# Two decoder blocks on one core: the convolutions' first tap moves from ACT to DVE, and the small table products go six to a step

## The chip, the core and the metric

The kernel runs on one core of a Trainium2 chip. The core has a matrix engine (PE, with its weight loads listed apart as PEld), a vector engine (DVE), a scalar engine (ACT), a general engine (POOL), and SyncE (SP), which here issues the DMAs of the weights. Each engine works through its own queue of instructions in the order in which they were written; between engines, an instruction waits on semaphores. The metric is the device time of one execution in microseconds, as the median of three runs.

## The reference

Two blocks are computed one after the other on a sequence of 256 tokens of width 2048, in fp32. The first block has two layers; the change lies mostly in its feed-forward network (FFN), which each layer has, and in its first mixer.

```python
def causal_dwconv(x, w):                  # CONV_WIDTH = 3
    s = x.shape[1]
    xp = jnp.pad(x, ((0, 0), (CONV_WIDTH - 1, 0), (0, 0)))
    y = xp[:, 0:s] * w[0]
    for j in range(1, CONV_WIDTH):
        y = y + xp[:, j:j + s] * w[j]
    return y

def short_conv_mixer(x, w_in, conv_w, w_out):
    b_gate, c_gate, xv = jnp.split(x @ w_in, 3, axis=-1)
    y = b_gate * causal_dwconv(c_gate * xv, conv_w)
    return y @ w_out

def conv_ffn(x, w_up, conv_w, conv_b, w_down):     # D_FF = 5632
    h = causal_dwconv(x @ w_up, conv_w) + conv_b
    g, u = jnp.split(h, 2, axis=-1)
    return (jax.nn.silu(g) * u) @ w_down

def first_block(...):
    for layer in range(2):
        mix = short_conv_mixer(...) if layer == 0 else diff_attention(...)
        x = layer_norm(ALPHA * x + mix, ...)
        x = layer_norm(ALPHA * x + conv_ffn(x, ...), ...)
    return x
```

The second block has an attention/linear-attention layer and a layer with a state-space mixer (S5). For the latter, tables are needed that depend on parameters alone (complex powers and their products with B and C); the kernel works them out early.

## The kernel before

**Tiles.** Activations lie transposed: 128 channels on the partitions, 256 tokens along the row, 16 such tiles for the width of 2048. A weight matrix is read in tiles of 128 x 128. Each fp32 operand is split into a high and a low part, so that a product becomes `hi` x (`xhi`, `xlo`) in one matmul of 512 columns (L308) and `lo` x `xhi` in one of 256 (L302). The splitting of the weights is done on the fly, per *unit* of 8 weight tiles: SP loads `raw` (L213), ACT makes `whi` (`hi_to`, an ACT copy of 128x1024, shown under the helper's line L195), DVE makes `wlo` (`lo_to`, L238). `raw` has 3 buffers, `whi` and `wlo` have 4 each. Before the matmuls of unit c are written, `whi` of unit c+2 is; after them, `wlo` of unit c+2 is. An output tile with 16 tiles of depth takes two units; 8 pairs of matmuls each.

**Epilogues.** What happens to an output tile after its matmuls is a generator: each `yield` ends a step, and one step of each waiting generator is written after each unit (`advance`). So a `yield` between two instructions puts them a unit apart in the program. `merge` (L482 to 487) takes the 512-wide PSUM tile: ACT copies the right half into `mt`, a step later DVE adds it to the left half (L487), which frees the PSUM tile; there are three such PSUM buffers (`pmm`). In an up tile of the FFN (`epi_up`) the sum goes into `pad`, one of four padded buffers; then comes the convolution `conv3`: the first tap on ACT (`h<-pad`, with weight and bias), a step later the second and third tap on DVE (L769, L770). The tiles alternate between gate and value: of a gate tile ACT takes the SiLU (`h<-h`), of a value tile DVE multiplies with the gate's (L1069), then `glu` is split, `hi` on ACT and, a step later, `lo` on DVE (L478). In the first mixer the convolution stands in `epi_xv`.

**FFN.** Each FFN goes through its 44 pairs of up tiles in three chunks (15, 15 and 14 pairs, `FCH`), and after each chunk the chunk's part of the down product (`mm_rows`): first four output tiles at once (`mm_side`, in groups of two depth tiles), then twelve one by one. A LayerNorm (`ln.apply`) stands ahead of each FFN.

**Background.** Other generators run beside: one step of each after every unit (`run_bg`). `s5_tables` is one of them, in the list `slow`, which pauses while a LayerNorm is near (`hold`). It has eight rounds (from L967), each of: complex products `cmul` (L899) of growing size, 1, 2, 4, 8, 16 and 32 columns for each of four channels, in steps of three or two DVE instructions; two times four instructions for `bd` (L981 to L984); twelve large products of 128x512 and 128x640 one to a step; transposes and products on PE, and copies on ACT.

Of the kernel before, what the change touches and what calls it, by code (L numbers as in the profile page):

```python
# [24 lines left out]
AF = mybir.ActivationFunctionType  # L25
OP = mybir.AluOpType
AX = mybir.AxisListType

T = 256
# [114 lines left out]
def kernel(ctx: ExitStack, tc: tile.TileContext, A, out, dbg=None, upto=99):  # L144
# [52 lines left out]
    V, S, G, PE = nc.vector, Scalar(), nc.gpsimd, nc.tensor  # L197
# [55 lines left out]
    def flush():  # L253
        while pending:
            advance()
# [168 lines left out]
    def P(name, i=0, n=1):  # L424
        c, w = COL[name]
        return par[:, c + i:c + i + n]
# [55 lines left out]
    def merge(ps, dst, m=128, mul=None, fac=None):  # L482

        t = ep.tile([128, T], F32, tag="mt", name="mt")
        S.activation(t[:m], ps[:m, T:], AF.Copy)
        yield
        V.tensor_add(dst, ps[:m, :T], t[:m])  # L487
        if mul is None:
            return
        while not mul.ready:  # L490
            yield
        if fac is None:
            V.tensor_mul(dst, dst, mul.rstd[:m])
        else:
            V.scalar_tensor_tensor(dst, dst, fac, mul.rstd[:m], op0=OP.mult, op1=OP.mult)
# [268 lines left out]

    def conv3(dst, pad, w, bias=0.0):

        S.activation(dst, pad[:, 0:T], AF.Identity, scale=w[0], bias=bias)
        yield
        V.scalar_tensor_tensor(dst, pad[:, 1:T + 1], w[1], dst, op0=OP.mult, op1=OP.add)  # L769
        V.scalar_tensor_tensor(dst, pad[:, 2:T + 2], w[2], dst, op0=OP.mult, op1=OP.add)  # L770

# [12 lines left out]
    cur = {}  # L784
# [7 lines left out]
    def epi_xv(i):  # L792
        def f(ps):
            z = ep.tile([128, T], F32, tag="c1", name="c1")
            yield from merge(ps, z)
            pad = pads[i % 4]
            V.tensor_mul(pad[:, 2:], z, cur.pop(("c", i)))
            cur["y", i] = ep.tile([128, T], F32, tag="c2", name="c2")
            yield from conv3(cur["y", i], pad, [P("a_conv", j * 16 + i) for j in range(3)])
        return f  # L800

    def epi_b(i):
# [80 lines left out]
    def s5_tables():  # L883
# [7 lines left out]
        def copy(dst, src, scale=1.0):  # L891
            S.activation(dst, src, AF.Copy, scale=scale)

        def cmul(dr, di, ar, ai, br, bi, u1, u2, n=3):

            ops = ((V.tensor_mul, u1, ar, br), (V.tensor_mul, u2, ai, bi), (V.tensor_sub, dr, u1, u2),
                   (V.tensor_mul, u1, ar, bi), (V.tensor_mul, u2, ai, br), (V.tensor_add, di, u1, u2))
            for i, (f, d, x, y) in enumerate(ops):
                f(d, x, y)  # L899
                if i % n == n - 1:  # L900
                    yield 1
# [65 lines left out]
        for i in range(8):  # L967
            bc = bgp.tile([128, 4, 4, 16], F32, tag="s5bc", name="s5bc", bufs=1)
            nc.gpsimd.dma_start(bc, A["s5bc"][:, i])
            p4 = slice(4 * i, 4 * i + 4)  # L970
            copy(d0[:, :, 1:], mag4[:, p4].unsqueeze(2).to_broadcast([128, 4, 63]))
            for k in range(6):
                n = 1 << k
                fr, fi = (pq[:, r, k, p4].unsqueeze(2).to_broadcast([128, 4, n]) for r in range(2))
                v1, v2 = u1[:, :, 0, :n], u2[:, :, 0, :n]
                yield from cmul(rot[:, 0, :, n:2 * n], rot[:, 1, :, n:2 * n], rot[:, 0, :, :n], rot[:, 1, :, :n],
                                fr, fi, v1, v2, 3 if n < 16 else 2)
            cr, ci = (z[:, p4].unsqueeze(2).to_broadcast([128, 4, 16]) for z in (cor, coi))
            w1, w2 = u1[:, :, 0, :16], u2[:, :, 0, :16]
            for r in range(2):  # L980
                V.tensor_mul(w1, cr, bc[:, r])  # L981
                V.tensor_mul(w2, ci, bc[:, 1 - r])
                for ps_, cs_ in half:
                    (V.tensor_add if r else V.tensor_sub)(bd[ps_, r, :, cs_], w1[ps_], w2[ps_])  # L984
                    copy(cd[ps_, r, :, cs_], bc[ps_, 2 + r])
                yield 1
            ar, ai = (pd[:, r, p4].unsqueeze(3).to_broadcast([128, 4, 4, 32]) for r in range(2))
            br, bi = (bd[:, r].unsqueeze(2).to_broadcast([128, 4, 4, 32]) for r in range(2))
            yield from cmul(ba[:, 0], ba[:, 1], ar, ai, br, bi, u1[:, :, :4], u2[:, :, :4], 1)
            for r in range(2):  # L990
                ps = pbg.tile([128, 4, 128], F32, tag="bg", name="s5t")
                for a in range(4):
                    PE.transpose(ps[:, a, :], ba[:, r, a].rearrange("p j h -> p (j h)"), ident)
                yield 1
                S.activation(bt[:, :, r, :], ps, AF.Copy)
            nc.sync.dma_start(s5_a[i], ta)
            ar, ai = (pa[:, r, p4].unsqueeze(3).to_broadcast([128, 4, 5, 32]) for r in range(2))
            br, bi = (cd[:, r].unsqueeze(2).to_broadcast([128, 4, 5, 32]) for r in range(2))
            yield from cmul(ca[:, 0], ca[:, 1], ar, ai, br, bi, u1, u2, 1)
            copy(ca[:, 1], ca[:, 1], -1.0)  # L1000
            yield 1
            for r, u in enumerate((u1, u2)):
                copy(u[:, :, :4], bd[:, r].unsqueeze(2).to_broadcast([128, 4, 4, 32]))
                yield 1
            yield 1
            ps = pbg.tile([128, 4, 128], F32, tag="bg", name="s5k")
            for a in range(4):
                for r in range(2):
                    PE.matmul(ps[:, a, :], (u1, u2)[r][:, a, :4].rearrange("p j h -> p (j h)"),
                              ca[:, r, a, :4].rearrange("p j h -> p (j h)"), start=r == 0, stop=r == 1)  # L1010
            yield 1
            for j in range(4):
                q = slice(32 * j, 32 * j + 32)
                S.activation(km[q, :, 32 * j:], ps[q, :, :128 - 32 * j], AF.Copy)
            nc.gpsimd.dma_start(s5_b[i][:, :1024].rearrange("p (r a j h) -> p r a j h", r=2, a=4, j=4),  # L1015
                                ca[:, :, :, 1:, :])
            nc.gpsimd.dma_start(s5_b[i][:, 1024:], km.rearrange("p a c -> p (a c)"))
            yield 1
# [28 lines left out]
    def ffn(layer, which, feed, scale=None):  # L1047
        r = big_r("rf")
        ln = LayerNorm(which, r)
        hold = {}  # L1050
        for f0, nf in FCH:
            glu = big_y("glu")

            def epi_up(j, i, is_u, glu):
                def f(ps):
                    pad = pads[(2 * i + is_u) % 4]
                    yield from merge(ps, pad[:, 2:])
                    if i == 0:
                        yield
                    h = ep.tile([128, T], F32, tag=f"c{is_u}", name="h")  # L1060
                    yield from conv3(h, pad, [P("f_conv", (layer * 3 + q) * 88 + j) for q in range(3)],
                          P("f_convb", layer * 88 + j))
                    if not is_u:
                        hold[i] = h
                        yield
                        S.activation(h, h, AF.Silu)
                        return
                    yield
                    V.tensor_mul(h, h, hold.pop(i))  # L1069
                    yield  # L1070
                    yield from split_late(glu, i, h)
                return f

            epis = [epi_up(f0 + i + NFF * u, i, u, glu) for i in range(nf) for u in range(2)]
            if f0:
                for e in epis:
                    mm_tile(xs, e)
            else:
                mm_run(xs, epis, feed)
                debug(f"ln{layer}", hres)  # L1080

            def epi_dn(m, f0=f0):
                def f(ps):
                    if f0 != FCH[-1][0]:
                        residual(r, m, ps, None if f0 == 0 else r)
                        return
                    ln.take(m, ps, r)
                    if m == 8:
                        S.tables()
                    if m < 14:  # L1090
                        yield
                    yield from ln.add(m, r)
                return f

            mm_rows(glu, epi_dn, f0, nf, ln.LAST if f0 == FCH[-1][0] else KT)
        flush()
        return ln.apply(xs, scale)
# [23 lines left out]
    scale = 128.0 ** -0.5  # L1121
# [617 lines left out]
    for e, a, n in ((V, 0, 1), (G, 5, 2), (V, 1, 2), (V, 3, 2), (G, 11, 2), (V, 7, 2), (V, 9, 2), (V, 13, 2), (V, 15, 1)):  # L1739
        y = hres[:, a:a + n, :]  # L1740
# [113 lines left out]
```

## Time and profile before

| | us |
|---|---|
| median of three runs (3296.56 to 3300.56) | 3298.67 |
| profiled execution | 3297.06 |
| its span, first to last instruction | 3295.3 |
| PE busy | 3215.1 |
| DVE busy | 2369.9 |
| ACT busy | 1710.7 |
| POOL busy | 484.7 |

The busy time of an engine is the time in which it had an instruction at work. A matmul that starts on time runs beside its neighbours, so a mean duration of one is longer than its share. "Idle before, releaser" tells how long an engine stood still before an instruction and whose end released it. The granted clock of PE is given as a share of full speed. The first FFN lies between about 404 and 1130 us of the span, the second between about 1612 and 2290.

### The profile page before, as it was taken

What the parts mean: (1) busy time and instruction counts of PE and PEld (TensorE: products, weight loads), DVE (VectorE), ACT (ScalarE), POOL (GpSimd) and SP (SyncE); (2) the same over time, 40 slices, a digit from 0 to 9 for tenths busy, and PEclk for the clock granted to TensorE, in tenths of its full rate; (3) what the DMA queues carried; (4) which work ended last, traced back from release to release, by engine and by line L of the source; (5) the groups of instructions that cost most, each with busy time, mean ns of one, the idle gap of its engine ahead of it and who ended that gap; (6) DMA issues with size and microseconds to landing.
All of it is one profiled execution on the core that took longest, in us unless ns stands there. A gap on an engine that the chain in (4) does not pass through costs nothing.

```text
span 3295.3 us, 51091 instructions
## 1 busy us (share of the span) xinstructions
PE 3215.1 (98%) x18674; PEld 2829.8 (86%) x18674; DVE 2369.9 (72%) x3958; ACT 1710.7 (52%) x2624; POOL 484.7 (15%) x551
## 2 busy tenths in 40 slices
PE   9999999999999999999999999999999999999998
PEld 8888887888888888888888888888788888899887
DVE  6677877777877785766866676667876666688765
ACT  5544555455455554554555455455554565444754
POOL 4200500000000066240500000000500001121102
PEclk9999999999999999999999999999999999999999
DMA  7666556666656646545466666666454555775554
GB/s 220 196 188 208 152 178 182 201 195 189 203 186 185 195 149 191 162 151 168 146 185 189 189 189 190 189 189 188 140 173 148 160 180 184 226 254 170 150 185 149
DMA packets 245131, 599.23 MB, mean 182 GB/s; under 512 B 36592, under 2 KB 119152, under 8 KB 244880
## 3 DMA queue, kind: packets, MB, share of 16 engines
q1 hardware_dynamic: 242496, 588.37, 58.4%
q0 software_dynamic: 2208, 7.37, 0.7%
q8 instruction: 147, 2.41, 0.3%
q14 instruction: 104, 0.85, 0.1%
q10 hardware_dynamic: 176, 0.23, 0.0%
HBM read 578.04 MB, written 17.83 MB: 181 GB/s over the span
## 4 chain that ended last, share of the span: by engine, by line
PE 76%; DVE 11%; DMA 4%; ACT 4%; issue 3%; SPq 1%; POOL 0%; DVEq 0%; ACTq 0%; POOLq 0%
PE mm L308 45%; PE mm L302 24%; DVE wlo L238 6%; ACT whi L195 3%; DMA raw<-in_up_dram 2%; DMA raw<-in_cd_dram 1%; PE ml L1302 1%; DVE h L769 1%; PE mm L305 1%; PE mm L395 1%; DVE pad L487 1%; PE mm L396 1%; PE mm L394 1%; SPq L213 1%; DMA raw<-in_a_in_dram 0%
## 5 line engine op out<-in xcount | busy, mean ns | idle before, releaser
L238 DVE TENSOR_TENSOR wlo<-raw,whi 128x1024 fp32r<-128x1024 f32 (+3 forms) x1083 | 1335.1, 1234 | 693.3 <-ACT whi L195 666.6
L308 PE MATMUL mm<-xs,whi 128*128 128x512 f32 x5776 | 1415.3, 394 | 18.2 <-DVE xs L650 11.0
L195 ACT ACTIVATE whi<-raw 128x1024 fp32r<-128x1024 f32 (+3 forms) x1083 | 1120.6, 1038 | 504.3 <-PE mm L308 225.6
L308 PEld LDWEIGHTS mm<-xs,whi 128*128 128x128 f32 x5776 | 1056.1, 189 | 227.0 <-issue 14.1
L302 PEld LDWEIGHTS mm<-xs,wlo 128*128 128x128 f32 x5776 | 751.2, 191 | 58.7 <-DVE wlo L238 25.8
L302 PE MATMUL mm<-xs,wlo 128*128 128x256 f32 x5776 | 779.1, 285 | 17.1 <-DVE wlo L238 15.6
L308 PE MATMUL mm<-glu,whi 128*128 128x512 f32 x1352 | 335.0, 394 | 12.2 <-DVE pad L487 9.4
L308 PEld LDWEIGHTS mm<-glu,whi 128*128 128x128 f32 x1352 | 247.9, 190 | 59.8 <-issue 13.8
L195 ACT ACTIVATE h<-pad,par 128x256 f32<-128x256 f32 x176 | 105.6, 601 | 369.8 <-DVE pad L487 365.5
L195 ACT ACTIVATE mt<-mm 128x256 f32<-128x256 f32 x369 | 136.5, 371 | 245.8 <-PE mm L308 224.6
L302 PEld LDWEIGHTS mm<-glu,wlo 128*128 128x128 f32 x1408 | 188.2, 193 | 11.6 <-DVE wlo L238 1.3
L302 PE MATMUL mm<-glu,wlo 128*128 128x256 f32 x1408 | 192.6, 285 | 1.1 <-DVE wlo L238 1.1
L1015 POOL DMA_DIRECT2D s5b<-s5ca x8 | 7.3, 910 | 776.8 <-ACT s5ca L195 776.8
L602 POOL COPY ln_s<-rf 128x256 f32<-128x256 f32 x2 | 0.9, 434 | 715.3 <-DVE rf L578 715.3
L770 DVE SCALAR_TENSOR_TENSOR h<-pad,par,h 128x256 f32<-128x256 f32 x176 | 85.4, 485 | 6.3
L769 DVE SCALAR_TENSOR_TENSOR h<-pad,par,h 128x256 f32<-128x256 f32 x176 | 84.2, 478 | 2.3 <-ACT h L195 2.3
L487 DVE TENSOR_TENSOR pad<-mm,mt 128x256 f32<-128x256 f32 x176 | 73.4, 418 | 2.9 <-ACT mt L195 2.9
L195 ACT ACTIVATE h<-h 128x256 f32<-128x256 f32 x88 | 36.7, 417 | 45.9 <-DVE h L770 45.5
L308 PE MATMUL mm<-y_att,whi 128*128 128x512 f32 x224 | 54.6, 391 | 0.0
L308 PE MATMUL mm<-y_cd,whi 128*128 128x512 f32 x224 | 54.5, 391 | 0.0
L308 PE MATMUL mm<-y_ab,whi 128*128 128x512 f32 x224 | 54.5, 391 | 0.0
L308 PE MATMUL mm<-y_conv,whi 128*128 128x512 f32 x224 | 54.5, 391 | 0.0
(566 smaller groups left out, 3151.6 us busy)
## 6 DMA issues: line engine op xcount, KB each, us to landing
raw<-in_up_dram SPq DMA_DIRECT2D x336, 512.0 KB, 3.9
raw<-in_ab_dram SPq DMA_DIRECT2D x106, 512.0 KB, 4.0
raw<-in_a_in_dram SPq DMA_DIRECT2D x88, 512.0 KB, 4.4
raw<-in_cd_dram SPq DMA_DIRECT2D x88, 512.0 KB, 4.4
raw<-in_down_dram SPq DMA_DIRECT2D x72, 512.0 KB, 3.8
raw<-in_down_dram SPq DMA_DIRECT2D x168, 128.0 KB, 2.6
raw<-in_down_dram SPq DMA_DIRECT2D x48, 448.0 KB, 4.0
raw<-in_k_dram SPq DMA_DIRECT2D x32, 512.0 KB, 4.4
```

Source lines behind the costliest of these rows:

```text
L195: nc.scalar.activation(dst, src, func, **k)
L213: nc.sync.dma_start(r[:, c:c + nk * m], w[t, :, k0:k0 + nk, :].rearrange("p k n -> p (k n)"))
L238: V.tensor_sub(lo[:, c:c + step], r[:, c:c + step], hi[:, c:c + step].bitcast(F32))
L302: PE.matmul(ps[:m, :T], lo[:, c:c + m], x[:, kx, :T], start=False, stop=last, skip_group_check=True)
L305: PE.matmul(ps[:m, :T], hi[:, c:c + m], x[:, kx, a:a + T], start=first and a == 0, stop=last and a == T, skip_group_check=True)
L308: PE.matmul(ps[:m, :], hi[:, c:c + m], x[:, kx, :], start=first, stop=last, skip_group_check=True)
L394: PE.matmul(ps[b], xhi, whi[:, :, k, :], start=first, stop=False, skip_group_check=True)
L395: PE.matmul(ps[b], xhi, wlo[:, :, k, :], start=False, stop=False, skip_group_check=True)
L396: PE.matmul(ps[b], xlo, whi[:, :, k, :], start=False, stop=last, skip_group_check=True)
L487: V.tensor_add(dst, ps[:m, :T], t[:m])
L769: V.scalar_tensor_tensor(dst, pad[:, 1:T + 1], w[1], dst, op0=OP.mult, op1=OP.add)
L770: V.scalar_tensor_tensor(dst, pad[:, 2:T + 2], w[2], dst, op0=OP.mult, op1=OP.add)
```

## The change

The first tap of every convolution (16 in the first mixer, 88 in each of the two FFNs) is no longer an ACT instruction but a `tensor_scalar` of DVE: multiplied with the weight, the bias (or zero) added. The step boundary behind it is gone: `conv3` is a plain function, and `pad`'s sum and the three taps stand in one step, so that what follows in the generator is written one unit earlier. In `s5_tables`, the products of 1, 2 and 4 columns take one step of six instructions where they took two of three, and the two halves of `bd` stand in one step: a round has 32 steps where it had 36. The number of table instructions is the same.

```diff
--- before.py
+++ after.py
@@ -764,8 +764,7 @@
 
     def conv3(dst, pad, w, bias=0.0):
 
-        S.activation(dst, pad[:, 0:T], AF.Identity, scale=w[0], bias=bias)
-        yield
+        V.tensor_scalar(dst, pad[:, 0:T], w[0], bias, op0=OP.mult, op1=OP.add)
         V.scalar_tensor_tensor(dst, pad[:, 1:T + 1], w[1], dst, op0=OP.mult, op1=OP.add)
         V.scalar_tensor_tensor(dst, pad[:, 2:T + 2], w[2], dst, op0=OP.mult, op1=OP.add)
 
@@ -796,7 +795,7 @@
             pad = pads[i % 4]
             V.tensor_mul(pad[:, 2:], z, cur.pop(("c", i)))
             cur["y", i] = ep.tile([128, T], F32, tag="c2", name="c2")
-            yield from conv3(cur["y", i], pad, [P("a_conv", j * 16 + i) for j in range(3)])
+            conv3(cur["y", i], pad, [P("a_conv", j * 16 + i) for j in range(3)])
         return f
 
     def epi_b(i):
@@ -974,7 +973,7 @@
                 fr, fi = (pq[:, r, k, p4].unsqueeze(2).to_broadcast([128, 4, n]) for r in range(2))
                 v1, v2 = u1[:, :, 0, :n], u2[:, :, 0, :n]
                 yield from cmul(rot[:, 0, :, n:2 * n], rot[:, 1, :, n:2 * n], rot[:, 0, :, :n], rot[:, 1, :, :n],
-                                fr, fi, v1, v2, 3 if n < 16 else 2)
+                                fr, fi, v1, v2, 6 if n < 8 else 3 if n < 16 else 2)
             cr, ci = (z[:, p4].unsqueeze(2).to_broadcast([128, 4, 16]) for z in (cor, coi))
             w1, w2 = u1[:, :, 0, :16], u2[:, :, 0, :16]
             for r in range(2):
@@ -983,7 +982,7 @@
                 for ps_, cs_ in half:
                     (V.tensor_add if r else V.tensor_sub)(bd[ps_, r, :, cs_], w1[ps_], w2[ps_])
                     copy(cd[ps_, r, :, cs_], bc[ps_, 2 + r])
-                yield 1
+            yield 1
             ar, ai = (pd[:, r, p4].unsqueeze(3).to_broadcast([128, 4, 4, 32]) for r in range(2))
             br, bi = (bd[:, r].unsqueeze(2).to_broadcast([128, 4, 4, 32]) for r in range(2))
             yield from cmul(ba[:, 0], ba[:, 1], ar, ai, br, bi, u1[:, :, :4], u2[:, :, :4], 1)
@@ -1058,7 +1057,7 @@
                     if i == 0:
                         yield
                     h = ep.tile([128, T], F32, tag=f"c{is_u}", name="h")
-                    yield from conv3(h, pad, [P("f_conv", (layer * 3 + q) * 88 + j) for q in range(3)],
+                    conv3(h, pad, [P("f_conv", (layer * 3 + q) * 88 + j) for q in range(3)],
                           P("f_convb", layer * 88 + j))
                     if not is_u:
                         hold[i] = h
```

ACT, first FFN, up tiles of the first chunk, before (`whi` is a unit's high weights, `mt` the PSUM half, `h<-pad` the first tap, `h<-h` the SiLU, `glu<-h` the high half of the product):

```order
L195 ACTIVATE whi<-raw 128x1024
L195 ACTIVATE mt<-mm 128x256
L195 ACTIVATE whi<-raw 128x1024
L195 ACTIVATE h<-pad_165,par 128x256
L195 ACTIVATE whi<-raw 128x1024
L195 ACTIVATE glu<-h 128x256
L195 ACTIVATE mt<-mm 128x256
L195 ACTIVATE whi<-raw 128x1024
L195 ACTIVATE h<-h 128x256
```

The same engine and chunk, after:

```order
L195 ACTIVATE whi<-raw 128x1024 x2
L195 ACTIVATE mt<-mm 128x256
L195 ACTIVATE whi<-raw 128x1024
L195 ACTIVATE glu<-h 128x256
L195 ACTIVATE whi<-raw 128x1024
L195 ACTIVATE h<-h 128x256
L195 ACTIVATE mt<-mm 128x256
L195 ACTIVATE whi<-raw 128x1024 x2
L195 ACTIVATE mt<-mm 128x256
```

The taps are gone, and with them what stood between two `whi` and waited for DVE's `pad`; the SiLU stands one unit earlier in its tile's course.

DVE, first FFN, end of the third chunk, before (`pad<-mm,mt` frees the PSUM tile; `s5u`, `s5ca` are table products):

```order
L238 TENSOR_TENSOR wlo<-raw,whi 128x1024
L769 SCALAR_TENSOR_TENSOR h<-pad_167,par,h 128x256
L770 SCALAR_TENSOR_TENSOR h<-pad_167,par,h 128x256
L899 TENSOR_TENSOR s5u_2230<-s5pa,s5cd 128x640
L238 TENSOR_TENSOR wlo<-raw,whi 128x1024
L1069 TENSOR_TENSOR h<-h 128x256
L487 TENSOR_TENSOR pad_169<-mm,mt 128x256
L899 TENSOR_TENSOR s5ca<-s5u_2229,s5u_2230 128x640
```

DVE at the end of the third chunk, after:

```order
L238 TENSOR_TENSOR wlo<-raw,whi 128x1024
L1068 TENSOR_TENSOR h<-h 128x256
L238 TENSOR_TENSOR wlo<-raw,whi 128x1024
L487 TENSOR_TENSOR pad_169<-mm,mt 128x256
L767 TENSOR_SCALAR h<-pad_169,par 128x256
L768 SCALAR_TENSOR_TENSOR h<-pad_169,par,h 128x256
L769 SCALAR_TENSOR_TENSOR h<-pad_169,par,h 128x256
L478 TENSOR_TENSOR glu<-h,glu 128x256
L487 TENSOR_TENSOR pad_171<-mm,mt 128x256
```

The two later taps stand right behind their own `pad` now, with the new first tap between, and no table product is left at this place.

DVE, first FFN, up tiles of the first chunk, before (the products of two columns, `128x4x2`):

```order
L238 TENSOR_TENSOR wlo<-raw,whi 128x1024
L769 SCALAR_TENSOR_TENSOR h<-pad_165,par,h 128x256
L770 SCALAR_TENSOR_TENSOR h<-pad_165,par,h 128x256
L899 TENSOR_TENSOR s5u_2229<-s5ta,s5pq 128x4x2
L899 TENSOR_TENSOR s5u_2230<-s5ta,s5pq 128x4x2
L899 TENSOR_TENSOR s5ta<-s5u_2229,s5u_2230 128x4x2
L238 TENSOR_TENSOR wlo<-raw,whi 128x1024
```

DVE, end of the first chunk, the products of two columns after:

```order
L238 TENSOR_TENSOR wlo<-raw,whi 128x1024
L1068 TENSOR_TENSOR h<-h 128x256
L898 TENSOR_TENSOR s5u_2229<-s5ta,s5pq 128x4x2
L898 TENSOR_TENSOR s5u_2230<-s5ta,s5pq 128x4x2
L898 TENSOR_TENSOR s5ta<-s5u_2229,s5u_2230 128x4x2
L898 TENSOR_TENSOR s5u_2229<-s5ta,s5pq 128x4x2
L898 TENSOR_TENSOR s5u_2230<-s5ta,s5pq 128x4x2
L898 TENSOR_TENSOR s5ta<-s5u_2229,s5u_2230 128x4x2
L238 TENSOR_TENSOR wlo<-raw,whi 128x512
```

Six small products stand between two `wlo` where there were three.

## Rows read from the trace of the kernel before

**Rows 1.** The page's part 1: busy us, share of the span, instructions.

```profile
PE 3215.1 (98%) x18674; PEld 2829.8 (86%) x18674; DVE 2369.9 (72%) x3958; ACT 1710.7 (52%) x2624; POOL 484.7 (15%) x551
```

**Rows 2.** Waits of PE, 404 to 1130: us in total, times, longest.

```profile
PE mm L302 <- DVE wlo L238: 13.8, 29, 1.8
PE mm L308 <- DVE pad L487: 6.9, 2, 3.7
PE mm L308 <- DVE s5u L899: 2.8, 1, 2.8
```

**Rows 3.** Waits of PE, 1612 to 2290.

```profile
PE mm L308 <- DVE pad L487: 2.5, 1, 2.5
PE mm L302 <- DVE wlo L238: 2.0, 2, 1.1
```

**Rows 4.** Stretches: PE, PEld, DVE, ACT, POOL busy; clock; DMA share; GB/s.

```profile
430.00:440.00 10.00, 8.36 (x41) 7.36 (x42) 7.92 (x14) 4.21 (x7) 0.00 (x0) 0.83 0.55 162
...
1100.00:1110.00 10.00, 7.02 (x26) 6.16 (x27) 8.31 (x15) 5.04 (x8) 0.00 (x0) 0.66 0.51 157
1780.00:1790.00 10.00, 6.46 (x35) 5.54 (x36) 7.46 (x15) 5.18 (x9) 0.00 (x0) 1.00 0.51 143
```

**Rows 5.** Instructions in time, 543 to 550: start, us, engine, form, [idle before].

```profile
543.75 0.42 DVE L487 TENSOR_TENSOR pad<-mm,mt 128x256 f32<-128x256 f32 x1
544.08 0.68 DVE L899 TENSOR_TENSOR s5u<-s5pd,s5bd 128x512 f32<-128x512 f32 x1
544.20 0.60 ACT L195 ACTIVATE h<-pad,par 128x256 f32<-128x256 f32 x1 [2.27 <-DVE pad L487]
...
544.71 1.04 ACT L195 ACTIVATE whi<-raw 128x1024 fp32r<-128x1024 f32 x1
545.65 0.36 ACT L195 ACTIVATE mt<-mm 128x256 f32<-128x256 f32 x1
545.78 1.23 DVE L238 TENSOR_TENSOR wlo<-raw,whi 128x1024 fp32r<-128x1024 f32 x1 [1.02 <-ACT whi L195]
...
546.93 0.48 DVE L769 SCALAR_TENSOR_TENSOR h<-pad,par,h 128x256 f32<-128x256 f32 x1
547.44 0.48 DVE L770 SCALAR_TENSOR_TENSOR h<-pad,par,h 128x256 f32<-128x256 f32 x1
...
549.91 0.41 DVE L487 TENSOR_TENSOR pad<-mm,mt 128x256 f32<-128x256 f32 x1
```

**Rows 6.** Stretches, as in rows 4: one tile with tables; up tiles without.

```profile
543.75:549.91 6.16, 5.81 (x33) 4.96 (x33) 5.10 (x9) 2.77 (x4) 0.00 (x0) 1.00 0.53 160
...
1900.00:1950.00 50.00, 50.00 (x289) 44.21 (x288) 35.21 (x54) 28.37 (x47) 0.00 (x0) 1.00 0.62 189
```

**Rows 7.** Waits of ACT over the span, as in rows 2.

```profile
ACT h L195 <- DVE pad L487: 365.5, 164, 3.8
...
ACT h L195 <- DVE h L770: 45.5, 75, 0.9
```

**Rows 8.** Instructions in time at the end of the third chunk, as in rows 5.

```profile
1098.63 0.61 PE L308 MATMUL mm<-glu,whi 128*128 128x512 f32 x2
...
1102.41 0.42 DVE L487 TENSOR_TENSOR pad<-mm,mt 128x256 f32<-128x256 f32 x1
1102.75 0.82 DVE L899 TENSOR_TENSOR s5ca<-s5u,s5u 128x640 f32<-128x640 f32 x1
...
1102.98 0.76 PE L308 MATMUL mm<-glu,whi 128*128 128x512 f32 x1 [3.74 <-DVE pad L487]
```

**Rows 9.** DVE's tensor_scalar with two scalars, two lines: ns min/median/max, first and last.

```profile
L1679 DVE TENSOR_SCALAR hg<-vz,lb x8: 399/406/821, 2894.5 to 3064.9; 128x256 f32<-128x256 f32 x8
...
L666 DVE TENSOR_SCALAR hres<-r,par x8: 695/816/830, 382.2 to 1611.8; 128x256 f32<-128x256 f32 x8
```

**Rows 10.** The stretch of all eight table rounds, line L899 alone: DVE busy.

```profile
202.00:1132.00 930.00, 122.28 (x384) 0.99 0.62 188
```

**Rows 11.** Groups of DVE: form, count, busy us, mean ns, idle before.

```profile
L984 DVE TENSOR_TENSOR s5bd<-s5u,s5u 64x64 f32<-64x64 f32 x32 | 7.0, 220 | 0.8
...
L899 DVE TENSOR_TENSOR s5u<-s5ta,s5pq 128x4 f32<-128x4 f32 x32 | 3.7, 158 | 0.0
```

## The prediction

> **What bounds the kernel now.** I read the page's busy shares first: PE is busy 98% of the span [rows 1], so only its idle time and its slow time are to be had; work moved between ACT and DVE costs or gains nothing unless PE waits for it. Then the waits of PE by releaser. In the first FFN (404 to 1130 us) PE waits 13.8 us for `wlo` in 29 pieces, and 9.7 us in three pieces for DVE work (`pad`, or a table product that stands beside it) [rows 2]; in the second FFN it is 2.0 and 2.5 us [rows 3]. That is 28.0 us. Where the largest of these lie, the granted clock falls: it is 0.83 over 10 us at 430 us (one of three such rows, with those at 570 and 840), and 0.66 at 1100, while at 1780 it stays at 1.00 [rows 4]. A mean of 0.83 over 10 us between the levels of 2.4 and 1.2 GHz loses 1.7 us of PE's work, 0.66 loses 3.4: 3 x 1.7 + 3.4 = 8.5 us. So 28.0 + 8.5 = 36.5 us is all that this change can reach; what PE waits for elsewhere (LayerNorm, attention) it doesn't touch.
>
> Then what makes `wlo` late, in order of time [rows 5]. DVE ends `pad` at 544.17, ACT takes the first tap (0.60, from 544.20), and only then, its queue being in order, the `whi` that stands behind the tap (1.04, from 544.71); DVE's next instruction is the `wlo` of that `whi`, so it stands idle 1.02 us, and starts at 545.78. Its taps follow, and the next `pad` starts at 549.91. One tile took 549.91 - 543.75 = 6.16 us, though DVE was busy for only 5.10 of them [rows 6]. PE alone, where nothing holds it, takes 50 us for 289 matmuls, 32 of them a tile: 5.54 us [rows 6]. So in these stretches the pace is set not by an engine but by a circle of hand-overs: `pad` (DVE), tap (ACT), `whi` (ACT), `wlo` (DVE), taps, `pad`. ACT's waits say the same: it waited 365.5 us for `pad`, 164 times, before a tap [rows 7].
>
> The long waits for `pad` are the same lateness at a chunk's end: PE begins the down product at 1098.63, gets through two matmuls, and stands until 1102.98, because the PSUM tile it needs next is only freed by the `pad` at 1102.41, late in DVE's queue [rows 8].
>
> **The first tap on DVE.** It removes 192 ACT instructions of 0.60 us (115 us of ACT, which is 52% busy: worth nothing in itself) and with them the circle: behind `whi` on ACT now stand only `mt`, `glu` and the SiLU. What it adds is a DVE instruction with two per-partition scalars. The nearest row is such a one on 128x256: 399 to 406 ns undisturbed [rows 9]. The other end is 816 ns, the same form inside a LayerNorm [rows 9], where POOL works beside it; in the stretches in question POOL's busy time is 0.00 [rows 4, 6], so I take 0.41. It also joins a chain: today `pad` is followed by an independent instruction that starts 0.33 us after it, 0.09 before its end, while a dependent tap starts 0.03 after the end of the one ahead (546.93 to 547.44 for 0.48) [rows 5]. Two dependent links instead of one overlap make 0.41 + 0.03 + 0.03 + 0.09 = 0.56 us. So the price t per tile lies between 0.41 and 0.56; I take 0.56.
>
> Does DVE then have room? Without tables it is busy 35.21 us of 50, which is 9.03 tiles, so 3.90 a tile [rows 6]; with the tap at most 4.46 of 5.54. In the second FFN nothing can be late for that. In the first FFN the tables lie on top. Their products take 122.28 us in eight rounds [rows 10], 15.3 a round, and L984 adds 7.0 in all; L981 and L982 have the same length and number between them [rows 11]: 14.0 / 8 = 1.75, so 17.0 a round.
>
> **The tables' steps.** One step runs after each unit (half a tile). A round has 36 steps; the change makes it 32 (three sizes take one step instead of two, the two halves of L981 to L984 one instead of two). Nothing is removed; 17.0 us now fall on 16 tiles instead of 18. The last round ends 32 units, some 90 us, earlier; in before it runs into the end of the last up chunk, where heavy products stand around the late `pad` [rows 8]. Six products of 0.16 [rows 11] make about 1 us in a step where there was 0.5, for three units of a round; a unit has (5.54 - 4.46) / 2 = 0.54 us to spare, so those three units put DVE back by some 1.4 us, and the joined L981 step (eight of 0.22) by another 1.2. Both are paid back in the steps of the round that have no DVE work (seven units).
>
> Sum for DVE in a round, all of it up tiles: 16 x (3.90 + t) + 17.0 = 86.0 us at t = 0.41 and 88.4 at 0.56, against PE's 16 x 5.54 = 88.6. So DVE is 97 to 100% full there, but has two to three units of lead to draw on (`lo_to` runs ahead of PE) and gets rest in the down stages, where no taps are. Before, it was 18 x 3.90 + 17.0 = 87.2 of 99.7, and lost PE's time by waiting. There DVE still sets the pace or nearly does, but by its own work and not by a round trip.
>
> By the Trainium skill (Perfetto Trace Analysis, Optimizing Scalar/DVE Operations) work that either engine can do should go to Scalar when DVE is saturated, the opposite of this change. The trace has DVE at 83% there and idle for a hand-over [rows 6], so I hold the rule to apply only if t turns out near the upper row; what that makes is the last rival.
>
> At the chunk ends, the order shows what stood ahead of the late `pad` in before: `wlo`, two taps, a table product of 0.82, `wlo`, a product of `h`. In the third chunk now only `wlo`, a product and `wlo` stand between an earlier tile's taps and that `pad`, since the tables are over by then. What holds `pad` then is `mt`, `whi` and `wlo` after the end of the tile before (0.36 + 1.04 + 1.23 [rows 5], some 3 us with the product), while PE has a whole tile of 5.54 to go: the wait goes. Late next would be the last tile's `glu`, which PE needs only in the last group of the down side, after some 56 pairs of matmuls: 56 x 5.54 / 16 = 19 us.
>
> **Sum.** Of 15.8 us of `wlo` waits I keep 4.0 (the stretch right after the LayerNorm, 410 to 432 us, where both engines are behind, and DVE's fullness); of 12.2 at chunk ends 1.5; of 8.5 us of clock 1.7 (one fall, after the LayerNorm). Gain 36.5 - 7.2 = 29.3 us. The profiled execution took 3297.06, its span being 3295.3; 3297.06 - 29.3 = 3267.8. The median of the runs lies 1.6 above the profiled one: 3269.
>
> **Rivals.** (1) *DVE is simply full.* The pads come in time, but `wlo` stays as late as it was in the first FFN (13.8 kept), and half the clock's loss with it (4.2), 1.5 at the chunk ends: gain 17.0, 3282. For it: 88.4 of 88.6. Against: the lead, and the rest in the down stages. (2) *The SiLU takes the tap's place*: it too waits on ACT for DVE, 45.5 us in 75 waits now [rows 7], and when DVE is fuller, its taps end later and `whi` is blocked as before. No gain: 3297, give or take 5. Against: the SiLU is issued a unit after the taps, behind the next `whi`, and stands in one tile of two. (3) *DVE becomes the bound*: slower. The `wlo` waits of before are 13.8 over some 4.7 rounds' worth of up tiles, 3.0 a round; DVE must overrun PE by more, so 16 x (3.90 + t) + 17.0 > 91.6, t > 0.76. If the tap costs the 0.82 of the upper row and 0.15 of links, t = 0.97: overrun 6.3 us a round, 4.5 rounds of up tiles with tables, 28 us; 13.8 and the 4.5 of the second FFN go, chunk ends and clock stay: 3297.06 + 28 - 18 + 1.6 = 3309. Against: no POOL work there.
>
> **Chances.** Forecast (gain 21 to 38) 0.59; (1) 0.18; (2) 0.12; (3) 0.11. 0.2% is 6.6 us, about what a measurement of this kernel can tell from no change. Forecast and (1) are faster: 0.77; (2) is the same, (3) slower. Low end: all 36.5 us gone gives 3262, and 3 for the spread of runs: 3259. High end: case (1) with the larger overrun, and the faster edge of (2): 3293.
>
> **What would show it.** Right: ACT's waits for `pad` gone, PE's waits for `wlo` in the first FFN under 5 us, no three-microsecond wait at 570, 840, 1100 and 1780, clock 1.00 there, the tap at about 0.41, DVE above 90% in up stretches with tables, the tables over near 1040 us. Wrong: the tap at 0.6 or more; PE's waits for `wlo` as many as before, with DVE busy right through them (1 or 3) or idle for `whi` behind a SiLU (2); or new waits in the attention or LayerNorm, which I take to be untouched.

## The result, and the profile after

The changed kernel takes 3255.74 us (median; 3254.76 to 3259.53) against 3298.48 for the kernel before in the same comparison: a ratio of 0.9872, 95% interval 0.9855 to 0.989. The forecast was 3269 with a range of 3259 to 3293: right in sign and in mechanism, too small by 13 us, and the time lies 3 us below the range. The profiled execution of the changed kernel took 3259.53 (span 3257.7), the longest of its four, so the stages below add up to 37.6 us and not to the 42.7 of the medians.

Where the time went, between the starts of the LayerNorms' statistics on PE (L613):

| stretch, us | before | after | difference |
|---|---|---|---|
| start to first LayerNorm (first mixer, with tables) | 373.8 | 374.9 | +1.1 |
| first FFN, with tables | 815.3 | 776.8 | -38.5 |
| attention | 408.5 | 411.8 | +3.3 |
| second FFN, no tables | 759.0 | 754.4 | -4.6 |
| rest | 938.7 | 939.8 | +1.1 |

A second profile of the changed kernel (3253.92 us) has -0.5, -40.1, +1.3, -6.2 and +2.3 us in these rows. So the gain lies in the two FFNs, and what the other stages gained or lost changes from profile to profile.

The page's busy shares, which answer to [rows 1], show the move: 95 us more on DVE, 78 less on ACT, and PE with the same 18674 matmuls and 15 us less busy.

```profile
PE 3199.9 (98%) x18674; PEld 2824.8 (87%) x18674; DVE 2464.9 (76%) x4150; ACT 1632.5 (50%) x2432; POOL 485.3 (15%) x551
```

Waits of PE from 404 to 1130 us (total, times, longest), where [rows 2] had 23.5 us in 32 pieces (one more of 0.5 us, for `whi`, is also gone and stands in no row there):

```profile
PE mm L302 <- DVE wlo L238: 1.8, 2, 1.6
PE mm L308 <- DVE pad L487: 1.7, 1, 1.7
```

Stretches (length, then PE, PEld, DVE, ACT, POOL busy, clock, DMA share, GB/s). The first four stand where the clock fell before, at 0.83, 0.83, 0.83 and 0.66 [rows 4]; it is 1.00 in all. The fifth is a stretch of up tiles with two table rounds, the last one without tables, as in [rows 6].

```profile
430.00:440.00 10.00, 10.00 (x59) 8.86 (x59) 9.82 (x17) 4.64 (x7) 0.00 (x0) 1.00 0.79 252
570.00:580.00 10.00, 10.00 (x57) 8.72 (x56) 7.82 (x16) 4.04 (x4) 0.00 (x0) 1.00 0.84 237
840.00:850.00 10.00, 10.00 (x58) 8.76 (x57) 7.69 (x17) 4.03 (x4) 0.00 (x0) 1.00 0.72 209
1100.00:1110.00 10.00, 10.00 (x61) 8.86 (x60) 6.98 (x12) 4.00 (x5) 0.00 (x0) 1.00 0.71 204
660.00:841.00 181.00, 181.00 (x1058) 160.27 (x1057) 163.97 (x324) 95.56 (x150) 3.99 (x6) 1.00 0.65 200
1900.00:1950.00 50.00, 50.00 (x289) 44.21 (x288) 39.66 (x63) 24.70 (x36) 0.00 (x0) 1.00 0.62 190
```

Of the kernel before, the stretch of 660 to 841 us (up tiles of the middle chunk with tables) reads:

```profile
660.00:841.00 181.00, 176.46 (x1014) 154.12 (x1014) 133.27 (x257) 100.94 (x167) 3.98 (x6) 1.00 0.62 190
```

In the same 181 us PE now gets through 1058 matmuls where it was 1014. DVE was busy for 74% of it and is now for 91%; ACT went from 100.94 to 95.56 us. At 1900 us PE's pace is the same 289 matmuls in 50 us in both kernels: in such a stretch without tables there was nothing to gain.

The tap is a DVE instruction of 0.41 us (ns: shortest, median, longest), which answers to [rows 9]; the 16 of the first mixer have no bias and are shorter:

```profile
L767 DVE TENSOR_SCALAR h<-pad,par x176: 404/414/579, 410.9 to 2236.6; 128x256 f32<-128x256 f32 x176
L767 DVE TENSOR_SCALAR c<-pad,par x16: 353/354/769, 35.6 to 280.4; 128x256 f32<-128x256 f32 x16
```

One tile of the third chunk in order of time (start, duration, engine; in brackets the idle time ahead of it), the counterpart of [rows 5] and, at its end, of [rows 8]:

```profile
1059.24 1.23 DVE L238 TENSOR_TENSOR wlo<-raw,whi 128x1024 fp32r<-128x1024 f32 x1 [1.04 <-ACT whi L195]
1059.43 2.08 PE L302 MATMUL mm<-xs,wlo 128*128 128x256 f32 x16
...
1060.39 0.42 DVE L487 TENSOR_TENSOR pad<-mm,mt 128x256 f32<-128x256 f32 x1
1060.84 0.41 DVE L767 TENSOR_SCALAR h<-pad,par 128x256 f32<-128x256 f32 x1
...
1061.35 3.82 PE L308 MATMUL mm<-xs,whi 128*128 128x512 f32 x16
...
1064.81 1.23 DVE L238 TENSOR_TENSOR wlo<-raw,whi 128x1024 fp32r<-128x1024 f32 x1 [1.04 <-ACT whi L195]
1065.00 2.08 PE L302 MATMUL mm<-xs,wlo 128*128 128x256 f32 x16
...
1066.91 2.00 PE L308 MATMUL mm<-xs,whi 128*128 128x512 f32 x8
...
1068.75 1.07 PE L308 MATMUL mm<-glu,whi 128*128 128x512 f32 x4
```

DVE goes from `pad` straight into the taps. It still stands idle 1.04 us for a `whi`, but PE does not: its sixteen L302 follow each other without a gap, 1065.00 - 1059.43 = 5.57 us after the last sixteen, and the down product at 1068.75 starts without the 3.74 us of [rows 8]. Here the idle DVE costs nothing, since `wlo` is ahead of PE; in [rows 5] the same idle second stood inside the circle that set the pace.

### The profile page after: what moved, and what is told of

Same layout as the page of the kernel before. It is cut to its first block, busy times and chain, and to the rows that moved or that the text cites. A ratio compares the mean times of both kernels' runs of the same rounds, so it can differ in the third digit from the quotient of the medians.

```text
span 3257.7 us, 51077 instructions
## 1 busy us (share of the span) xinstructions
PE 3199.9 (98%) x18674; PEld 2824.8 (87%) x18674; DVE 2464.9 (76%) x4150; ACT 1632.5 (50%) x2432; POOL 485.3 (15%) x551
## 4 chain that ended last, share of the span: by engine, by line
PE 85%; DVE 7%; DMA 3%; issue 1%; ACT 1%; SPq 1%; POOL 0%; DVEq 0%; ACTq 0%; POOLq 0%
PE mm L308 51%; PE mm L302 27%; DVE wlo L238 3%; DMA raw<-in_cd_dram 1%; PE ml L1301 1%; ACT whi L195 1%; SPq L213 1%; DMA raw<-in_up_dram 1%; PE mm L395 1%; PE mm L396 1%; PE mm L394 1%; DMA raw<-in_a_in_dram 1%; DVE r L578 0%; DVE rf L578 0%; PE s5k L1008 0%
## 5 line engine op out<-in xcount | busy, mean ns | idle before, releaser
L308 PE MATMUL mm<-xs,whi 128*128 128x512 f32 x5776 | 1411.6, 393 | 17.0 <-DVE xs L650 9.8
L308 PEld LDWEIGHTS mm<-xs,whi 128*128 128x128 f32 x5776 | 1054.6, 188 | 223.7 <-issue 11.7
L302 PEld LDWEIGHTS mm<-xs,wlo 128*128 128x128 f32 x5776 | 748.2, 191 | 37.6 <-DVE wlo L238 4.8
L302 PE MATMUL mm<-xs,wlo 128*128 128x256 f32 x5776 | 768.7, 284 | 3.4 <-DVE wlo L238 3.3
L308 PE MATMUL mm<-glu,whi 128*128 128x512 f32 x1352 | 331.3, 392 | 1.7 <-DVE pad L487 1.7
L308 PEld LDWEIGHTS mm<-glu,whi 128*128 128x128 f32 x1352 | 245.8, 188 | 47.8 <-issue 2.1
L302 PEld LDWEIGHTS mm<-glu,wlo 128*128 128x128 f32 x1408 | 185.5, 191 | 11.6 <-DVE wlo L238 1.8
L302 PE MATMUL mm<-glu,wlo 128*128 128x256 f32 x1408 | 190.0, 283 | 1.6 <-DVE wlo L238 1.6
L195 ACT ACTIVATE h<-h 128x256 f32<-128x256 f32 x88 | 36.8, 418 | 128.0 <-DVE h L769 128.0
L767 DVE TENSOR_SCALAR h<-pad,par 128x256 f32<-128x256 f32 x176 | 73.5, 417 | 5.9
L195 ACT ACTIVATE glu<-h 128x256 fp32r<-128x256 f32 x88 | 36.1, 411 | 50.7 <-DVE h L1068 50.4
L606 POOL TENSOR_TENSOR ln_s<-ln_s,ln_q 128x256 f32<-128x256 f32 x52 | 55.2, 1062 | 0.0
L308 PE MATMUL mm<-y_att,whi 128*128 128x512 f32 x224 | 54.7, 392 | 0.0
L308 PE MATMUL mm<-y_cd,whi 128*128 128x512 f32 x224 | 54.5, 391 | 0.0
## 6 DMA issues: line engine op xcount, KB each, us to landing
raw<-in_down_dram SPq DMA_DIRECT2D x168, 128.0 KB, 2.6
```

Source lines behind the costliest of these rows:

```text
L195: nc.scalar.activation(dst, src, func, **k)
L302: PE.matmul(ps[:m, :T], lo[:, c:c + m], x[:, kx, :T], start=False, stop=last, skip_group_check=True)
L308: PE.matmul(ps[:m, :], hi[:, c:c + m], x[:, kx, :], start=first, stop=last, skip_group_check=True)
L606: E.tensor_add(self.s2, self.s2, q)
L767: V.tensor_scalar(dst, pad[:, 0:T], w[0], bias, op0=OP.mult, op1=OP.add)
```

## Experiments

The names: theory C says that the circle `pad`, tap, `whi`, `wlo` was what cost the time, T that the tables' shorter course is what helps, S that the step boundary matters and not the engine, W that `whi` is late for another reason than the tap ahead of it. "Before" is run beside each.

**The taps alone.** The change's `conv3`, the tables as before:

```diff
-        S.activation(dst, pad[:, 0:T], AF.Identity, scale=w[0], bias=bias)
-        yield
+        V.tensor_scalar(dst, pad[:, 0:T], w[0], bias, op0=OP.mult, op1=OP.add)
```

> The first taps on DVE in one step with the later ones; the tables keep the steps of before (36 a round). Theory C (what is gained is the circle pad on DVE, tap on ACT, whi on ACT, wlo on DVE): nearly all of the gain, 3260 us give or take 6, PE's waits for wlo in the first FFN under 5 us; the tables still end near 1100 us, but no heavy product makes PE wait there, since pad comes in time. Rival T (the gain comes from the tables, which end earlier and are clear of the chunk ends): less than 15 us of gain, 3284 or more, with waits for pad at the chunk ends left.

Measured: 3251.21 us (3250.12 to 3252.74), ratio 0.9859 (0.9844 to 0.9874). The taps are the whole gain, and some 4 us more than the change as it stands. The time is 3 us below C's range. In the first FFN PE has no listed wait for `wlo` or `pad`, not even at the end of the third chunk, though the table products are still at work there (the last ends at 1072.7 us):

```profile
1062.89 0.82 DVE L898 TENSOR_TENSOR s5ca<-s5u,s5u 128x640 f32<-128x640 f32 x1
...
1063.84 1.07 PE L308 MATMUL mm<-glu,whi 128*128 128x512 f32 x4
1064.51 0.42 DVE L487 TENSOR_TENSOR pad<-mm,mt 128x256 f32<-128x256 f32 x1 [0.47 <-ACT mt L195]
...
1065.21 1.09 PE L308 MATMUL mm<-glu,whi 128*128 128x512 f32 x4
```

**The tables alone.** The first tap on ACT as before, the tables in 32 steps:

```diff
-                                fr, fi, v1, v2, 3 if n < 16 else 2)
+                                fr, fi, v1, v2, 6 if n < 8 else 3 if n < 16 else 2)
...
-                yield 1
+            yield 1
```

> The tables in 32 steps a round, the first tap on ACT as before. Theory C: the circle stays. A tile without table work takes 6.16 - 2 x 0.60 = 4.96 us of it, so a round takes 16 x 4.96 + 15.5 = 95 us against PE's 88.6, 6 us lost a round in 4.5 rounds of up tiles (before: 5 in 4.7): about 4 us more of waits, and the wait and the slow clock at the third chunk's end (3.7 + 3.4) gone: 3295 us give or take 5. Rival T: 3270 to 3285.

Measured: 3294.2 us (3289.81 to 3299.21), ratio 0.9989 (0.998 to 0.9998). PE's waits from 404 to 1150 us are nearly those of [rows 2]:

```profile
PE mm L302 <- DVE wlo L238: 16.5, 31, 1.5
PE mm L308 <- DVE pad L487: 7.3, 3, 3.6
```

T falls: without the taps the tables' part is worth some 4 us (0.7 to 6.6 by the interval). The time is in C's range, but not by C's reckoning: the wait at the third chunk's end, which it had gone, is still 2.74 us, though the last table product ends at 1019.6 us, far ahead of it. The one that shrank is the middle chunk's (2.8 us before; here 0.99, with 1.11 for `wlo` behind it).

```profile
1098.54 0.61 PE L308 MATMUL mm<-glu,whi 128*128 128x512 f32 x2
1101.90 1.19 PE L308 MATMUL mm<-glu,whi 128*128 128x512 f32 x2 [2.74 <-DVE pad L487]
```

**The tap on DVE, the step boundary kept** (tables as changed), so that the second and third tap still come a unit later:

```diff
         V.tensor_scalar(dst, pad[:, 0:T], w[0], bias, op0=OP.mult, op1=OP.add)
+        yield
```

> The changed kernel, but with the step boundary between first and second tap kept, so that all that follows in the epilogue is written a unit later, as before. Theory C: within 6 us of the changed kernel, 3250 to 3262. Rival S (the shorter epilogue makes the gain): half of the gain or less, 3277 or more.

Measured: 3251.84 us (3249.27 to 3252.83), ratio 0.9858 (0.9841 to 0.9874). It is the engine, not the boundary; S falls.

**The circle opened at another place.** The kernel before, with ACT's `whi` written one unit further ahead, so that it stands ahead of the tap it had been blocked by; the tap stays on ACT and DVE gets no work:

```diff
-        hi_to(c + (4 if st["hold"] else 3 if c else 2))
+        hi_to(c + (4 if c else 2))
```

> The kernel before with one number changed: ACT makes whi one unit further ahead (of unit c+3 instead of c+2 ahead of unit c's matmuls); taps and tables as before. Then the whi that DVE's next wlo needs stands ahead of the tap in ACT's queue, and the circle is open though the tap stays on ACT. Theory C: most of the gain without the change, 3258 to 3272, PE's waits for wlo in the first FFN under 6 us. Rival W (it is ACT's or DVE's load, or the epilogue's length): no gain, 3293 or more.

Measured: 3257.09 us (3253.92 to 3261.26), ratio 0.9877 (0.9862 to 0.9892). The time is 1 us below C's range. The first FFN takes 772.9 us, as with the taps alone (773.0); the 6 us by which the whole is slower than they are lie outside it. Its row of 660 to 841 us has the full pace with DVE at 81% and ACT busier than in any other version:

```profile
660.00:841.00 181.00, 181.00 (x1056) 160.23 (x1055) 147.39 (x292) 109.11 (x178) 3.98 (x6) 1.00 0.65 198
```

This is the best evidence for C: the tap is on the same engine as before, and the first FFN's lost time is gone once the `whi` that is needed next no longer stands behind it. W, here the load of ACT or DVE or the length of the epilogue, falls. By itself the run would fit any other reason for a late `whi` too; that it is the tap is seen in [rows 5] and in the taps alone.

**The changed kernel once more**, beside the next three, since it lay 4 us behind its own taps alone.

> The changed kernel once more, as the measure for the other three. Beside it the taps-alone kernel took 3251.2 and the one that keeps the step boundary 3251.8, the changed kernel 3255.7. If the 4 us are the program's own (theories P and Q below): 3254 to 3258, with some 20 matmuls fewer between 540 and 580 us than the other two have (213 against 232 to 234), that is 3.4 us. If they were the chip's or the hour's: 3250 to 3253.

Measured: 3256.07 us (3253.92 to 3258.99), ratio 0.9869 (0.9856 to 0.9883). So the 4 us are the program's own. The place is the end of the first chunk. Of the changed kernel, 540 to 580 us, and its PE and DVE there:

```profile
540.00:580.00 40.00, 36.67 (x213) 32.01 (x214) 32.95 (x76) 19.77 (x32) 1.71 (x3) 1.00 0.68 199
```

```profile
561.27 0.61 PE L308 MATMUL mm<-glu,whi 128*128 128x512 f32 x2
561.39 0.24 DVE L898 TENSOR_TENSOR s5u<-s5ta,s5pq 128x8 f32<-128x8 f32 x2
...
562.41 0.69 DVE L238 TENSOR_TENSOR wlo<-raw,whi 128x512 fp32r<-128x512 f32 x1
563.02 0.42 DVE L487 TENSOR_TENSOR pad<-mm,mt 128x256 f32<-128x256 f32 x1
...
563.59 0.70 PE L308 MATMUL mm<-glu,whi 128*128 128x512 f32 x2 [1.71 <-DVE pad L487]
...
566.07 0.42 DVE L487 TENSOR_TENSOR pad<-mm,mt 128x256 f32<-128x256 f32 x1
566.53 0.41 DVE L767 TENSOR_SCALAR h<-pad,par 128x256 f32<-128x256 f32 x1
...
567.90 1.22 DVE L238 TENSOR_TENSOR wlo<-raw,whi 128x1024 fp32r<-128x1024 f32 x1
...
569.17 0.74 PE L302 MATMUL mm<-glu,wlo 128*128 128x256 f32 x4 [1.62 <-DVE wlo L238]
```

Two steps of six small products and the taps of a tile stand ahead of the `pad` that frees PE's PSUM tile, and two pads with all their taps ahead of the next `wlo`. The kernel that keeps the boundary has 232 matmuls in that row, the taps alone 234, the changed kernel in this second profile 219 (the first is shown): 13 to 21 matmuls fewer, which at 181 / 1058 = 0.171 us are 2.2 to 3.6 us.

**The same tables, one round 20 us later** (the changed kernel with a pause of seven units ahead of the fourth round):

```diff
         for i in range(8):
+            if i == 3:
+                yield 7
```

> The changed kernel, with a pause of seven units ahead of the fourth table round, nothing else. Theory P: the 4 us that the changed kernel loses against its own taps alone lie at the end of the first chunk, because there the round's small products, six to a step, meet three pads and their taps that PE waits for (1.71 us for pad at 563.59, 1.62 for wlo at 569.17); with the round 20 us later the two waits are gone: 3250 to 3253. Theory Q: six products to a step cost PE's time wherever they stand, and the joined steps of the round too: 3255 to 3258.

Measured: 3252.69 us (3251.47 to 3253.52), ratio 0.9859 (0.9844 to 0.9874), and from 404 to 1130 us only 1.1 us of waits:

```profile
PE mm L302 <- DVE wlo L238: 1.1, 2, 0.9
```

So six products to a step cost next to nothing by themselves; what costs is that a round begins with them at the very end of a chunk. The taps in one step with `pad` have a part in it as well, since the kernel that keeps the boundary, with the same tables, does not lose there. Theory P holds, Q falls.

**The first tap twice** (the changed kernel, the `tensor_scalar` issued a second time), to see what room DVE has:

```diff
         V.tensor_scalar(dst, pad[:, 0:T], w[0], bias, op0=OP.mult, op1=OP.add)
+        V.tensor_scalar(dst, pad[:, 0:T], w[0], bias, op0=OP.mult, op1=OP.add)
```

> The changed kernel with the first tap issued twice (the second overwrites the first with the same values): 0.41 us and a link of 0.03 more for each of 192 tiles on DVE. Theory B, by the sum of the prediction: 16 x (3.90 + 0.56 + 0.44) + 17.0 = 95.4 us of DVE in a round against PE's 88.6, an overrun of 6.8 a round, 3.4 to 5 rounds of up tiles: 3276 to 3288, DVE at 99% in the up stretches and PE waiting for wlo. Theory F, by the changed kernel's trace: DVE was busy for 163.97 of 181 us (660 to 841), and 32.7 tiles x 0.44 = 14.4 more make 178.4, so it still fits: 3255 to 3264.

Measured: 3279.38 us (3277.79 to 3284.4), ratio 0.9941 (0.9929 to 0.9954). The time is B's, and theory F, read from a DVE share of 91%, falls. But the picture is not quite B's either, and its sum took 88.6 us for a round of PE, which left out the tables' matmuls (below), so that the time came into its range in part by luck: PE's waits are back, and DVE is at 93% there (167.86 of 181), not at 99%.

```profile
PE mm L302 <- DVE wlo L238: 14.4, 20, 2.5
PE mm L308 <- DVE pad L487: 2.2, 1, 2.2
```

```profile
660.00:841.00 181.00, 177.37 (x1020) 155.41 (x1019) 167.86 (x336) 89.04 (x138) 2.90 (x4) 1.00 0.62 192
```

The 93% are a mean of full and of waiting stretches. From 754 to 812 us DVE has no listed wait and is busy for 55.94 us of 58, 96%, and there PE waits four times for `wlo`: DVE is full.

```profile
754.00:812.00 58.00, 55.76 (x319) 48.45 (x318) 55.94 (x127) 25.90 (x43) 0.00 (x0) 1.00 0.56 172
```

```profile
PE mm L302 <- DVE wlo L238: 2.2, 4, 1.3
```

In the rest of the 181 us it waits 7.9 us for `whi` in nine pieces of up to 2.0. One like these, of 2.00 us at 470.60, comes of four table copies of 1.74 us that stand ahead of `whi` on ACT, and ahead of them of a SiLU for which ACT had stood idle 1.80 us until DVE's last tap was done: that is the wait of the prediction's rival (2). How much of the lost time is DVE's own work and how much these waits was not taken apart. In the changed kernel 91% over this stretch left little room: 0.44 us a tile more took back over half of what the change had won. In the second FFN, without tables, the doubled tap costs little (755.1 us against 754.4).

**Both ways of opening the circle** (the taps alone, and `whi` a unit further ahead):

> The taps alone on DVE, and ACT's whi one unit further ahead as well: two ways to open the same circle, together. Theory C (only the circle was to be had; either edit opens it): nothing on top, 3249 to 3254, as the taps alone with 3251.2. Theory E (each of them leaves some lateness that the other takes): 3240 to 3247.

Measured: 3259.67 us (3258.68 to 3264.7), ratio 0.9883 (0.9869 to 0.9896): neither theory had it slower than the taps alone. Against `whi` ahead alone (3253.92 to 3261.26) the ranges overlap. The first FFN is the shortest of all (771.9 us, no wait of PE for `wlo` or `pad`), so C's "nothing more to be had" is right there. The profiled execution, at 3264.7 the slowest of its four, loses its time elsewhere, against that of the taps alone: 4.0 us ahead of the first LayerNorm, 2.5 in the attention, 2.7 in the second FFN, 5.3 in the rest. In the first of these the wait of PE that grew is for the low half of `xs` (L478); this kernel's row of 0 to 380 us, and then that of the taps alone:

```profile
PE mm L308 <- DVE xs L478: 7.1, 3, 4.5
```

```profile
PE mm L308 <- DVE xs L478: 3.5, 2, 2.7
```

With `whi` further ahead, ACT stands longer at the head of its queue for PE to give a `whi` buffer back, and does nothing else meanwhile; with the taps alone this is 251.8 us in 246 waits, with `whi` ahead alone 871.5 in 521, here

```profile
ACT whi L195 <- PE mm L308: 963.3, 577, 8.9
```

That this is what delays the other stages was not tried by itself and stays open.

## Where the prediction was right, and the step that failed

**What bounds the kernel: right.** Two edits that have nothing in common but the circle (the tap's engine; the place of `whi`) bring the first FFN from 815.3 to 773 us, and another, the tables alone, leaves it at 810.6. ACT's 365.5 us of waits for `pad` [rows 7] are gone with the tap.

**The tap's price: right.** 0.41 us for the instruction. Without tables DVE's time goes from 35.21 [rows 6] to 39.66 us in 9.03 tiles, 0.49 a tile, between the 0.41 and 0.56 of the prediction. The 0.82 of the upper row [rows 9] did not come in the FFNs, where the longest tap took 0.58; one tap of the first mixer took 0.77.

**DVE's fullness: the term was too high, the warning right.** 97 to 100% were forecast and 91% measured in a stretch of two rounds. The tables were priced well: their products (L898 of the changed kernel) are busy 30.47 us there, and the four lines of `bd` 3.5, together the 17.0 a round of the sum.

```profile
660.00:841.00 181.00, 30.47 (x95) 1.00 0.65 200
```

Three things made the sum too high: PE's side, 88.6 us a round, left out the tables' own matmuls (48 in this stretch, 6.3 us, so 3.2 a round); the tap was taken at 0.56, not 0.49; and added durations count twice what neighbours on DVE overlap (0.09 us of a `pad` in [rows 5]). The first two give 87.2 of 91.8, 95%; the rest, some 4 us a round by this estimate, falls to the third. But the doubled tap shows how near the edge that still was: it meets what rival (1), "DVE is simply full", describes. That its 3279 us lie near the 3282 given for that rival is chance, since those were reckoned for a single tap.

**Chunk ends: the third's wait goes, but not for the reason given; the first was not looked at.** The prediction let the third run through "since the tables are over by then". The runs show the tap as the reason: with the taps alone the tables are still at work there and PE does not wait, and with the tables alone they end some 80 us ahead of that place and it waits 2.74 us. At the first chunk's end, 3.3 us of waits are left (before it was one of 3.2, with a fall of the clock), where the prediction kept 1.5 for all chunk ends: the six products to a step, named there as a cost that is paid back, meet a place where it isn't. The change loses 3 to 4 us by it, as the round that starts later shows.

**The clock: right.** It is 1.00 in all four rows, so the 8.5 us are back. The fall that the prediction kept, behind the LayerNorm, is not the same in each profile; in this one of the changed kernel it is deeper than before, which leaves 8.5 - 25 x (0.93 - 0.86) = 6.8 us. Before, then after:

```profile
375.00:400.00 25.00, 20.92 (x121) 18.15 (x122) 23.73 (x30) 15.15 (x27) 12.40 (x15) 0.93 0.38 110
```

```profile
375.00:400.00 25.00, 21.10 (x117) 18.44 (x118) 23.79 (x30) 14.18 (x26) 12.39 (x15) 0.86 0.35 104
```

In the second profile of the changed kernel it is 0.93 again, and the 8.5 us remain.

**Rival (2), the SiLU: its wait came, not its effect.** ACT waits 128.0 us for the last tap in 82 pieces now (45.5 in 75 before, [rows 7]), but PE's waits did not follow.

**The sum: this is the step that failed.** It took the waits of PE by releaser, 28.0 us, and 8.5 us of clock as "all that this change can reach". In the second profile, whose clock behind the LayerNorm is that of before, 25.9 of these waits and the 8.5 are gone, 34.4 us, where the forecast counted on 29.3. But the two FFNs became 40.1 + 6.2 = 46.3 us shorter. The missing 12 us, 10 of them in the first FFN, are in no row of waits, since a wait cost more here than the idle time that its row shows. It can be seen in one late `wlo` of the kernel before:

```profile
548.25 1.11 PE L302 MATMUL mm<-xs,wlo 128*128 128x256 f32 x8
549.72 1.22 PE L302 MATMUL mm<-xs,wlo 128*128 128x256 f32 x8 [0.35 <-DVE wlo L238]
550.77 1.55 PE L308 MATMUL mm<-xs,whi 128*128 128x512 f32 x6
```

Undisturbed, sixteen L302 take 1066.91 - 1065.00 = 1.91 us to the next start, eight take 0.96, as the tile above (of the changed kernel) shows. Here eight take 549.72 - 548.25 = 1.47, so 0.51 us is lost, and the row says 0.35: the last matmul before the gap counts as busy to its end (548.25 + 1.11), 0.15 us beyond the 0.96 after which a neighbour would have started. The next eight need 1.05 us until L308 starts, another 0.09. (The starts alone give the 0.51; how it divides rests on the matmuls' ends, which the profile models.) That makes 0.25 us for one wait beyond its row, and [rows 6] had it: 6.16 us for a tile against 5.54 is 0.62 lost, of which the trace shows 0.35 as idle.

The runs give the same by other ways, always first FFN against first FFN. Before against after: 38.5 - 20.0 (waits) - 6.8 (clock) = 11.7 us in 29 waits more, 0.40 each; against the second profile 40.1 - 21.4 - 8.5 = 10.2 us in 30, 0.34 each. The doubled tap against the change: 800.0 - 776.8 = 23.2, less 13.1 of waits and 3.2 of clock (0.83 for 1.00 from 850 to 860 us, 0.80 for 0.86 from 375 to 400), 6.9 us in 18 waits more, 0.38 each. In the stretch of 660 to 841 us: 44 matmuls at 0.171 are 7.5 us, PE's idle time is 4.5 and nine waits are named: 0.33 each. Had the sum been made by pace (5.54 us a tile against what a tile takes), these 10 us and more would have been in it, and the range's low end would have lain at 3249 or lower, below the 3255.7 that came.

**A smaller slip.** The profiled execution and the median were set 1.6 us apart, as they were before; after, they stand 3.8 apart to the other side. This offset is a run's chance and not a property of a kernel.

By the Trainium skill (Perfetto Trace Analysis, Optimizing Scalar/DVE Operations), when DVE is saturated it may make sense to move work that both engines can do from it to Scalar; the prediction had made a "should" of this. The runs agree, with the condition read from more than a mean share: at 74% in the row of 660 to 841 us DVE took the tap and the kernel gained 1.3%, because DVE had been idle for a hand-over; at 91% another 0.44 us a tile cost 0.7%, and the mean over that row then was no more than 93%.

**A version that beats both.** The taps alone (3251.2), the boundary kept (3251.8) and the round started later (3252.7) are all some 3 to 5 us ahead of the changed kernel, ranges not overlapping the 3253.92 to 3259.53 of its runs. Between the three the runs don't tell a difference.

## What to carry to other kernels

Where PE waits many times for a short while, take what can be won from the pace (time of a tile against the time of a tile that nothing holds), not from the sum of its waits: here the waits and the clock showed three quarters of it. Where an instruction on a second engine stands between two of a first, look at what stands behind it in the second engine's queue, and whether the first waits for that in turn. A mean share of 91% can leave little room in an engine that is fed by hand-overs, since full stretches and waits are both in it; and a background that begins a heavy step is best kept away from the ends of the stages that it runs beside, as the round moved by 20 us shows.

## What the runs showed of the hardware that was not expected

The duration of DVE's `tensor_scalar` on 128x256 in fp32 depends on its scalars: 354 ns (median) with one scalar per partition and a constant (the first mixer's taps), 414 ns with two (the FFNs' taps); the 816 ns of [rows 9], with two, show that this holds for undisturbed ones alone. And a wait of PE in this kernel cost 0.25 to 0.40 us beyond the idle time in its row, in the comparisons above.
